# Laying the normalised activations out anew in place, by cycles of chunk copies, instead of building them three times

## The chip, the cores and the metric

The kernel runs on one core of one Trainium2 chip. The metric is the device time of one execution in microseconds, the median over several executions.

## The reference, cut to what matters

One layer takes 2048 prompt tokens and 64 decode tokens (8 sequences of 8). The activations are normalised and multiplied by one wide matrix; of the product, twelve heads of q, k and v go to attention. The heads are in three groups of four, with dilations 1, 4 and 16: a query sees its own token and 128 earlier ones, each `dil` apart. The three groups are merged by the softmax of their log-sums. A gated linear recurrence runs beside it, and both branches are gated, projected and added to the input.

```
u = rms_norm(x, g_norm);  z = u @ w_in            # xa, ga, q, k, v, gb, gm
for g, dil in enumerate((1, 4, 16)):              # per class t % dil, blocks of 128 tokens
    s = q_blk @ [k_prev, k_blk].T * scale + bias[dist]     # band of 129
    o[g], lse[g] = softmax(s) @ [v_prev, v_blk], logsumexp
ob = sum_g softmax_g(lse)[g] * o[g];  yb = (ob * silu(gb)) @ w_attn_proj
h = scan(a * h + b);                  ya = (h * silu(ga)) @ w_lru_proj
y = x + (sig(gm1) * ya + sig(gm2) * yb) @ w_out
```

## The kernel before, in words

All matmuls are in float32r with operands split into a high and a low part. The normalised activations stand transposed in SBUF as `RH` and `RL` (high and low part): 128 partitions, 8 slices of the model dimension, 2112 token columns. They are 16 blocks of 128 prompt tokens and one of 64 decode tokens.

**Order of work.** The program is written out by hand in the order in which each engine is to run it. The attention loop (L536) goes over 204 units: twelve heads, groups 2, 1, 0 (dilations 16, 4, 1), and per head 16 prompt blocks and one decode block. Below, *head n* is the n-th in this order (heads 0 to 3 have dilation 16, 4 to 7 dilation 4, 8 to 11 dilation 1), and `ph` is the unit's place in its head. A unit runs through stages spread over four iterations: projection `z` of the block (`stage_a`, 24 matmuls in three parts), then norms (`stage_b1` to `b3`; the scale `rs` comes from two small POOL operations, L347 and L348), transposes of k and q (`stage_c`), scores and softmax (`stage_d`), transposes of the probabilities (`stage_e`), their product with v (`stage_f`), and the sum into tile `o` (`stage_g`, DVE), which SP writes to the DRAM buffer `Osc` (L435). After a head's last block, SP gathers the softmax statistics from `Osc` into `STt` (L437).

**Layout.** A block must be 128 tokens of one class modulo `dil`, in order. So before groups 1 and 0 the whole array is made anew during the last head of the group before (heads 3 and 7): per unit one block of x is loaded (L225), multiplied by scale and weight (`x_mul`, L241, two DVE operations), transposed on PE (`x_tr`, L248, eight 128x128 transposes) and split into `RH` and `RL` (L94 on ACT, L95 on DVE, two of each).

**Beside it.** The decode path's scores against the K cache (`kgo`: two DVE reductions L179 per step, 128 steps for a group) run inside the loop: group 2's in heads 4 to 6, group 1's in heads 8 to 11. The K tiles come over SP's queue. Weights are loaded a head ahead in four `wraw` buffers (L305) and split (L312 to L324); the bias band `T3` is read from DRAM (L298, L299).

After the loop come the attention gates (L534), the recurrence (L763 with L864 and L926; eight blocks), gate matmuls, and the output projections (L1425, L1481, L1513).

Of the kernel before, what the change touches and what calls it, by code (L numbers as in the profile page):

```python
# [42 lines left out]
def program(tc, I, O, C, upto=99, debug=False):  # L43
# [21 lines left out]
    RS = sd("RS", [SEQ])  # L65
# [18 lines left out]
    RH = rp.tile([128, 8, NT], F32R, name="RH")  # L84
    RL = rp.tile([128, 8, NT], F32R, name="RL")
# [117 lines left out]
    xrs = ap_.tile([128, 2, 17], F32, name="xrs")  # L203
    xt = {}

    def x_open():
# [3 lines left out]
        if G.again:  # L210
            x_load(1)
# [3 lines left out]
    def xv(j):  # L215
        if j == 16:
            return I["x_sample"].rearrange("b t d -> (b t) d")
        d = DIL[G.xg]
        r, n = divmod(j, 16 // d)
        return I["x_prompt"][0, n * 128 * d + r:min(n * 128 * d + r + 128 * d, SEQ):d, :]  # L220

    def x_load(j):
        if j < (17 if G.xg == 2 and not G.again else 16):
# [3 lines left out]
    def x_norm(j):  # L227
# [4 lines left out]
        POOL.tensor_tensor(xrs[0:p, 0, j:j + 1], ss[0:p, 1:2], neghalf[0:p, 0:1], ALU.pow)  # L232

    def x_scales():
        dma(raw(RS, 0, [[16, 128], [1, 16]]), xrs[:, 0, 0:16])
        dma(xrs[:, 1, 0:16], raw(RS, 0, [[4, 128], [1, 4], [512, 4]]))
        dma(xrs[:, 0, 0:16], raw(RS, 0, [[1, 128], [128, 16]]))

    def x_mul(j, a=0, b=D):
        p = 128 if j < 16 else NS  # L240
        DVE.scalar_tensor_tensor(xt[j][0:p, a:b], xt[j][0:p, a:b], xrs[0:p, G.xg % 2, j:j + 1], G.gn[0:p, a:b], ALU.mult, ALU.mult)  # L241

    def x_tr(j, i):
# [115 lines left out]
    def stage_b3(u):  # L359
# [7 lines left out]
        if u.smp:  # L367
            dma(SK[u.g, :, :, u.h, :], u.kvo[0:m])
            dma(QS[u.g, :, u.h * HD:(u.h + 1) * HD], u.qn[0:m, :])
        elif u.out is not None:  # L370
            dma(u.out, u.kvo)
# [12 lines left out]
    def stage_d(u):  # L384
# [11 lines left out]
        u.o = ap_.tile([128, 130], F32, name="o", tag="o", bufs=3)  # L396
# [1206 lines left out]
```

## Time and profile before

| | us |
|---|---|
| median of 3 runs | 2517.61 (2517.22 to 2520.73) |
| the profiled execution | 2513.91 |
| its span, first to last instruction | 2512.1 |
| PE busy | 2477.1 (99%) |
| DVE busy | 1544.1 (61%) |
| ACT busy | 1083.5 (43%) |
| POOL busy | 565.1 (22%) |

Busy shares are taken over the span. Matmuls are pipelined, so that several are in flight at once and the durations of single ones add up to more than PE's time. DMA-issuing instructions of SP are not counted as busy.

### The profile page before, as it was taken

Reading aid. Unit: us, or ns where it says so; the run is one execution under the profiler, and the core shown is the slowest. Engines: PE = TensorE matmul, PEld = TensorE weight load, DVE = VectorE, ACT = ScalarE, POOL = GpSimd, SP = SyncE. Lnnn points to the kernel's source line nnn. Section 1 sums busy time; section 2 is a strip of 40 time slices with the busy share of each in tenths; the row PEclk is TensorE's granted clock in tenths of the full one; section 3 lists DMA queues with packets and bytes.
Section 4 is the critical chain, followed back from the end, with each engine's and each line's share of the span. In section 5 each row is a group of like instructions: output and inputs, shape, how many; then the busy total and the mean of one; then the engine's idle time right before and its main releaser. Section 6 shows DMA issues by size and latency. Waiting matters only on the chain.

```text
span 2512.1 us, 44593 instructions
## 1 busy us (share of the span) xinstructions
PE 2477.1 (99%) x15178; PEld 2333.8 (93%) x15178; DVE 1544.1 (61%) x4805; ACT 1083.5 (43%) x3318; POOL 565.1 (22%) x901
## 2 busy tenths in 40 slices
PE   8999999999999999999999999999999999999999
PEld 7999999999999999999998989998998899989988
DVE  6744687777786777746567767766776633423323
ACT  5634454443444434444355566546566511211110
POOL 3423322222212212223324334340000112200000
PEclk9999999999999999999999999999999999999999
DMA  5453565555553443426644433445654489533332
GB/s 146 119 131 106 148 186 148 167 172 144 163 171 112 132 122 99 124 81 203 202 155 139 147 103 120 143 126 187 201 195 154 151 262 328 169 118 122 110 120 67
DMA packets 310824, 376.30 MB, mean 150 GB/s; under 512 B 55360, under 2 KB 254943, under 8 KB 307756
## 3 DMA queue, kind: packets, MB, share of 16 engines
q1 hardware_dynamic: 283604, 336.12, 44.2%
q0 software_dynamic: 15472, 20.02, 3.0%
q10 hardware_dynamic: 11520, 17.31, 1.9%
q8 instruction: 120, 1.97, 0.3%
q14 instruction: 108, 0.88, 0.1%
HBM read 295.45 MB, written 168.33 MB: 185 GB/s over the span
## 4 chain that ended last, share of the span: by engine, by line
PE 87%; DMA 4%; DVE 3%; ACT 2%; issue 2%; POOL 1%; SPq 0%; ACTq 0%; POOLq 0%; DVEq 0%
PE z L336 28%; PE zt L763 28%; PE zt L1481 8%; PE zt L1513 7%; PE zt L1425 3%; PE zt L534 3%; PE zga L891 2%; PE trx L248 1%; PE op L428 1%; PE S L406 1%; PE tre L416 1%; PE trc L376 1%; DMA wr<-in_w_in 1%; DMA xt<-in_x_prompt 1%; PE trc L377 1%
## 5 line engine op out<-in xcount | busy, mean ns | idle before, releaser
L336 PE MATMUL z<-w,RH 128*128 128x384 f32 (+1 forms) x3088 | 888.9, 349 | 4.9 <-POOL w L317 1.8
L763 PE MATMUL zt<-RH,wz 128*128 128x384 f32 (+2 forms) x2560 | 695.5, 354 | 0.0
L336 PEld LDWEIGHTS z<-w,RH 128*128 128x128 f32 (+1 forms) x3088 | 553.1, 188 | 14.8 <-POOL w L317 5.9
L336 PE MATMUL z<-w,RL 128*128 128x384 f32 x1544 | 520.3, 337 | 0.1
L763 PEld LDWEIGHTS zt<-RH,wz 128*128 128x128 f32 x2560 | 463.3, 189 | 43.1 <-issue 1.0
L763 PE MATMUL zt<-RL,wz 128*128 128x384 f32 (+2 forms) x1280 | 452.5, 353 | 0.0
L336 PEld LDWEIGHTS z<-w,RL 128*128 128x128 f32 x1544 | 291.3, 189 | 0.8 <-DVE RL L95 0.5
L763 PEld LDWEIGHTS zt<-RL,wz 128*128 128x128 f32 x1280 | 241.3, 189 | 22.2
L179 DVE CUSTOM_DVE_ANT_0 kjk<-kt,qs 128x128 bf16<-128x128 f32 x768 | 227.5, 296 | 37.0 <-DMA kt<-in_cache_kv_w 13.8
L408 ACT ACTIVATE P<-P,o 128x128 f32<-128x128 f32 (+1 forms) x192 | 88.9, 463 | 312.8 <-DVE o L407 312.8
L345 ACT ACTIVATE jk<-z 128x128 bf16<-128x128 f32 (+1 forms) x408 | 113.0, 277 | 249.9 <-PE trc L376 185.0
L347 POOL TENSOR_SCALAR ss<-ss 128x2 f32<-128x2 f32 (+1 forms) x204 | 45.1, 221 | 705.2 <-ACT jk L345 666.7
L95 DVE TENSOR_TENSOR KQ<-trc,KQ 128x256 fp32r<-128x256 f32 x192 | 81.4, 424 | 198.2 <-ACT KQ L94 198.2
L1481 PEld LDWEIGHTS zt<-y1t,w_wlo 128*128 128x128 f32 x1536 | 190.3, 191 | 0.6
L1481 PE MATMUL zt<-y1t,w_wlo 128*128 128x256 f32 (+1 forms) x1536 | 190.6, 286 | 0.0
L1513 PE MATMUL zt<-w_wo,mt 128*128 128x512 f32 x672 | 162.0, 395 | 0.0
L1513 PEld LDWEIGHTS zt<-w_wo,mt 128*128 128x128 f32 x672 | 126.0, 188 | 30.7
L348 POOL TENSOR_TENSOR rs<-ss,neghalf 128x2 f32<-128x2 f32 (+1 forms) x204 | 142.8, 700 | 17.0
L94 ACT CAST mt<-g 128x256 fp32r<-128x256 f32 x72 | 27.2, 388 | 191.2 <-DVE g L1484 176.0
L434 DVE TENSOR_REDUCE o<-op 128x128 f32<-128x256 f32 x192 | 80.5, 419 | 44.8 <-PE op L429 44.7
L1515 DVE TENSOR_TENSOR xr<-zt,xr 128x512 f32<-128x512 f32 (+1 forms) x34 | 23.5, 692 | 137.2 <-PE zt L1513 132.5
L1150 ACT ACTIVATE v<-v,P 128x128 f32<-128x128 f32 x256 | 80.1, 390 | 47.1 <-DVE SCk L179 23.2
(291 smaller groups left out, 4247.1 us busy)
## 6 DMA issues: line engine op xcount, KB each, us to landing
out_kv_s<-in_cache_kv_w SPq DMA_DIRECT2D x176, 480.0 KB
xt<-in_x_prompt SPq DMA_DIRECT2D x48, 512.0 KB
wr<-in_w_in SPq DMA_DIRECT2D x96, 192.0 KB
kt<-in_cache_kv_w SPq DMA_DIRECT2D x128, 128.0 KB
wzr<-in_w_in SPq DMA_DIRECT2D x32, 512.0 KB
v<-in_cache_kv_w SPq DMA_DIRECT2D x128, 128.0 KB
Osc<-o SPq DMA_DIRECT2D x192, 65.0 KB
ot<-Osc SPq DMA_DIRECT2D x32, 390.0 KB
```

The costliest lines, as they stand in the source:

```text
L95: eng.tensor_sub(l, src, h.bitcast(F32))
L179: DVE.tensor_tensor_reduce(jk, kts[q.tile][:, c], qts[t][:, c], 1.0, 0.0, ALU.mult, ALU.add, q.SC[:, o:o + 1])
L336: PE.matmul(u.z[0:m, :], (RH, RL, RH)[p][:, k, u.cols], Wt[(u.g, u.h), k][:, (0, 0, 1)[p], :], start=(i == 0), stop=(i == 23))
L345: ACT.activation(jk[0:m, :], z[0:m, i * 128:(i + 1) * 128], AF.Square, accum_out=u.ss[0:m, i:i + 1])
L348: POOL.tensor_tensor(u.rs[0:m, :], u.ss[0:m, :], neghalf[0:m, :], ALU.pow)
L408: ACT.activation(u.P[:, 0:n], u.P[:, 0:n], AF.Exp, bias=u.o[:, 128:129], scale=-1.0, accum_out=u.o[:, 129:130])
L434: DVE.tensor_reduce(u.o[:, 0:128], u.op.rearrange("p a b -> p b a"), AX.X, ALU.add)
L534: PE.matmul(z[0:m, 0:256], (RH, RH, RL)[p][:, k, j * 128:j * 128 + m], wb[c * 8 + k][:, (0, 1, 0)[p], :], start=(i == 0), stop=(i == 23))
L763: PE.matmul(z[:, 0:n], w[:, (0, 1, 0)[p], k, :], (RH, RH, RL)[p][:, k, c0:c0 + n], start=(i == 0), stop=(i == 23))
L1150: ACT.activation(v2s[n][:, h], v2s[n][:, h], AF.Copy, scale=P2[:, h, n:n + 1])
L1481: PE.matmul(z[:, 0:n], wl[k][:, (0, 1, 0)[p], f, :], y1s[c * 8 + k][:, (0, 0, 1)[p], 0:n], start=(i == 0), stop=(i == 23))
L1513: PE.matmul(z[0:m, :], ms_[k][:, (0, 0, 384)[p] + o:(0, 0, 384)[p] + o + m], wo[k][:, (0, 1, 0)[p], e * 4:(e + 1) * 4, :].rearrange("p k c ...
```

## The change

The array is loaded, scaled and transposed once. `RH` and `RL` become two views of one tile `RX`. Blocks start in the order of dilation 16 with classes 0, 4, 8, 12, 1, 5, ... For dilation 4, and later for dilation 1, chunks of 32 columns (of all 16 slices of high and low part: 512 elements in each partition) are moved in place: 24 exchanges of two chunks (three copies each, 72) in head 3, and 20 cycles of three chunks (four copies each, 80) in head 7 and the first units of head 8. Each cycle starts with a POOL copy into one of four spare tiles; in exchanges DVE makes the other two copies, in cycles of three ACT, DVE and ACT make the other three. Up to five copies are issued in a unit (two, two, one).

The tokens of a block stay permuted within it. The bias band is therefore read with permuted rows and its columns are permuted by a POOL copy (`bias_p`), two units after the read and some units earlier than before; k and v outputs go out in parts; `Osc` holds rows in the permuted order of dilation 1; the recurrence un-permutes on ACT's way into `xpad` and permutes on POOL's product L926; x and y are read and written with permuted rows. The `o` tiles of dilation 4 are written by four POOL DMAs (32 rows each), issued one unit later, or at once after a head's last block. The K-cache steps begin at iterations 73 and 149 instead of 71 and 139, and the second lot runs two per place throughout.

```diff
-    RH = rp.tile([128, 8, NT], F32R, name="RH")
-    RL = rp.tile([128, 8, NT], F32R, name="RL")
+    RX = rp.tile([128, 2, 8, NT], F32R, name="RX")
+    RH, RL = RX[:, 0], RX[:, 1]
...
-        return I["x_prompt"][0, n * 128 * d + r:min(n * 128 * d + r + 128 * d, SEQ):d, :]
+        return I["x_prompt"][0, j // 4 + 4 * (j % 4):SEQ:16, :]
...
+    def chunk(g, blk, n):
+        v = RX.rearrange("p s k t -> p (s k) t")[:, :, blk * 128:blk * 128 + 128]
+        if g == 1:
+            return v[:, :, n * 32:n * 32 + 32]
+        return v.rearrange("p k (c n i) -> p k c n i", c=4, n=4)[:, :, :, n]
...
+    def queue(g, blk):
+        for c in cycles(g, blk):
...
+            def first(c=c, t=t):
+                v = G.xp.tile([128, 16, 32], F32R, name="mv", tag="mv", bufs=4)
+                t.append(v if g == 1 else v.rearrange("p k (c i) -> p k c i", c=4))
+                cp(POOL, t[0], chunk(g, *c[-1]))
+            fs = [first]
+            for n in range(len(c) - 1, 0, -1):
+                fs.append(lambda n=n, c=c: cp((ACT, DVE)[n % 2], chunk(g, *c[n]), chunk(g, *c[n - 1])))
+            fs.append(lambda c=c, t=t: cp((DVE, ACT)[len(c) % 2], chunk(g, *c[0]), t[0]))
+            moves.extend((min(b for b, n in c), f) for f in fs)
+        moves.sort(key=lambda m: m[0])
...
+    def bias_p(g, h):
+        if g != 2:
+            A = PA[g]
+            t = ap_.tile([128, 384], F32, name="T3", tag="T3", bufs=2)
+            POOL.tensor_copy(t.rearrange("p (n a b) -> p n a b", a=A, b=128 // A), Tt[g, h].rearrange("p (n b a) -> p n a b", a=A, b=128 // A))
...
-        u.o = ap_.tile([128, 130], F32, name="o", tag="o", bufs=3)
+        u.o = ap_.tile([128, 130], F32, name="o", tag="o", bufs=4)
...
+    def flush_o():
+        if G.late:
+            G.late()
+            G.late = None
     def stage_g(u):
...
+        flush_o()
         DVE.tensor_reduce(u.o[:, 0:128], u.op.rearrange("p a b -> p b a"), AX.X, ALU.add)
-        dma(Osc[u.g, u.tok, u.h, :], u.o)
...
+            G.late = lambda: [POOL.dma_start(raw(Osc, b + (u.blk % 4 * 512 + (4 * a + u.r) * 8) * st, [[128 * st, 4], [st, 8], [1, 130]]), u.o[a * 32:a * 32 + 32]) for a in range(4)]
         if u.last:
+            flush_o()
...
-            kgo(2 if i < 136 else 1 + (i % 2 == 0))
+            kgo(2)
...
-            if i > 50 and i // 17 in (3, 7) and ph:
-                x_mul(ph - 1, D // 2, D)
-                x_tr(ph - 1, 0)
+            move(2)
             stage_a(u, 1)
...
-                x_tr(ph - 1, 1)
-                x_load(ph + 1)
+            move(2)
             stage_a(u, 2)
+            if i // 17 in (3, 7) and ph < 16:
+                queue(1 if i < 68 else 0, ph)
...
-                x_mul(ph, 0, D // 2)
+            move(1)
...
-        ACT.copy(xpad[:, 3 + c0:3 + c0 + npr], z[:, 0:npr])
+        ACT.copy(xpad[:, 3 + c0:3 + c0 + npr].rearrange("p (n k x) -> p n x k", k=8, x=16), z[:, 0:npr].rearrange("p (n x k) -> p n x k", k=8, x=16))
```

## Rows read from the trace of the kernel before

**Rows 1.** The page, section 1: busy us, share of the span, instructions.
```profile
PE 2477.1 (99%) x15178; PEld 2333.8 (93%) x15178; DVE 1544.1 (61%) x4805; ACT 1083.5 (43%) x3318; POOL 565.1 (22%) x901
```
**Rows 2.** The page, section 4: the chain that ended last, shares by line.
```profile
PE z L336 28%; PE zt L763 28%; PE zt L1481 8%; PE zt L1513 7%; PE zt L1425 3%; PE zt L534 3%; PE zga L891 2%; PE trx L248 1%; PE op L428 1%; PE S L406 1%; PE tre L416 1%; PE trc L376 1%; DMA wr<-in_w_in 1%; DMA xt<-in_x_prompt 1%; PE trc L377 1%
```
**Rows 3.** Windows, line 376 alone (one per unit): stretch, length, PE busy (count).
```profile
213.25:298.49 85.24, 4.61 (x17) 2.35 (x17) 1.00 0.44 121
```
**Rows 4.** Windows, heads 2 to 7: PE, PEld, DVE, ACT, POOL busy, clock, DMA.
```profile
213.25:298.49 85.24, 84.94 (x525) 82.63 (x524) 43.98 (x157) 35.51 (x162) 25.88 (x54) 1.00 0.44 121
298.49:399.07 100.58, 98.17 (x639) 94.31 (x638) 81.34 (x214) 50.50 (x191) 25.93 (x53) 1.00 0.61 175
399.07:488.30 89.23, 89.10 (x565) 87.52 (x564) 65.48 (x317) 36.97 (x160) 21.08 (x42) 1.00 0.57 168
488.30:579.47 91.17, 89.66 (x566) 87.55 (x565) 69.09 (x333) 37.07 (x160) 20.95 (x42) 1.00 0.53 158
579.47:672.31 92.84, 90.21 (x573) 88.36 (x572) 63.88 (x289) 38.36 (x162) 21.43 (x42) 1.00 0.54 162
672.31:776.84 104.53, 103.32 (x687) 100.40 (x686) 81.96 (x202) 53.14 (x191) 21.78 (x42) 1.00 0.53 152
```
**Rows 5.** Windows, tile trx alone (the x transposes), heads 3 and 7.
```profile
298.49:399.07 100.58, 18.59 (x120) 12.59 (x120) 21.20 (x31) 17.30 (x30) 1.00 0.61 175
...
672.31:776.84 104.53, 18.32 (x120) 13.06 (x120) 21.19 (x31) 17.30 (x30) 1.00 0.53 152
```
**Rows 6.** Timeline into iteration 116: start, us, engine, line, operation, [idle before, releaser].
```profile
644.72 1.01 DVE L95 TENSOR_TENSOR w<-wr,w 128x384 fp32r<-128x384 f32 x1
...
646.41 0.19 POOL L347 TENSOR_SCALAR ss<-ss 128x2 f32<-128x2 f32 x1 [1.10 <-ACT jk L345]
...
646.62 0.42 DVE L95 TENSOR_TENSOR KQ<-trc,KQ 128x256 fp32r<-128x256 f32 x1 [0.89 <-ACT KQ L94]
646.69 0.69 POOL L348 TENSOR_TENSOR rs<-ss,neghalf 128x2 f32<-128x2 f32 x1
...
647.60 0.34 DVE L363 SCALAR_TENSOR_TENSOR kvo<-z,rs,gk 128x128 f32<-128x128 f32 x1
647.63 0.28 PE L399 MATMUL S<-KQ 128*128 128x256 f32 x1
...
650.59 0.27 PE L376 MATMUL trc<-ident,kvo 128*128 128x128 f32 x1
```
**Rows 7.** Groups by line and form: count | busy us, mean ns | idle before.
```profile
L179 DVE CUSTOM_DVE_ANT_0 kjk<-kt,qs 128x128 bf16<-128x128 f32 x768 | 227.5, 296 | 37.0 <-DMA kt<-in_cache_kv_w 13.8 <-DMA qs<-QS 1.2 <-DMA out_h_s<-hs 0.2
L95 DVE TENSOR_TENSOR RL<-trx,RH 128x512 fp32r<-128x512 f32 x96 | 66.4, 691 | 39.4 <-ACT RH L94 39.0
L1154 DVE COPY V<-v 128x512 f32<-128x512 f32 x1 | 0.4, 408 | 0.0
L882 ACT CAST xh<-xc 128x512 fp32r<-128x512 f32 x16 | 10.0, 625 | 33.2 <-DVE xc L873 33.2
L907 POOL TENSOR_TENSOR a<-rr 128x512 f32<-128x512 f32 x16 | 16.3, 1042 | 56.3 <-ACT rr L905 48.9 <-issue 7.4
L926 POOL TENSOR_TENSOR sgl<-sgl,tt 128x512 f32<-128x512 f32 x16 | 24.5, 1533 | 32.4 <-DVE tt L925 32.4
L1135 POOL DMA_DIRECT2D PSC<-pp x8 | 4.4, 572 | 53.7 <-DVE pp L1132 53.7
L758 POOL DMA_DIRECT2D Y<-yt x16 | 12.1, 756 | 10.0 <-ACT yt L94 6.1 <-ACT ob L739 3.0 <-ACT sg L712 0.8
```
**Rows 8.** DMA issues: operation, count, KB each, median us to landing.
```profile
PSC<-pp POOLq DMA_DIRECT2D x8, 16.0 KB, 3.9
```
**Rows 9.** The chain in order of time, end of head 4: start, us, what.
```profile
489.90 4.80 DMA Osc<-o
```
**Rows 10.** Windows, one block of the recurrence: same columns as rows 4.
```profile
1291.67:1343.24 51.57, 51.57 (x272) 46.97 (x271) 36.63 (x50) 30.93 (x54) 20.15 (x20) 1.00 0.43 140
```
**Rows 11.** Source view of line 144: durations ns min/median/max, first and last start.
```profile
L144 SPq DMA_DIRECT2D qs<-QS x16: 605/606/662, 775.3 to 786.2; - x16
```

More of the change, by code (lines that the diff above doesn't have):

```diff
@@ L217, in xv @@
             return I["x_sample"].rearrange("b t d -> (b t) d")
[L218 to L220 removed]
+        return I["x_prompt"][0, j // 4 + 4 * (j % 4):SEQ:16, :]
     def x_load(j):
[L223 removed]
+        if j < 17:
             xt[j] = G.xp.tile([128, D], F32, name="xt", tag="xt", bufs=2)
@@ L253, in x_tr, with cycles, move, cp @@
             POOL.tensor_copy(XS[:, i * 4:i * 4 + 4, 1], RL[s].bitcast(F32))
+    PA = (16, 4)
+    moves = []
+    def chunk(g, blk, n):
[3 more added lines that the diff above has]
+        return v.rearrange("p k (c n i) -> p k c n i", c=4, n=4)[:, :, :, n]
+    def cycles(g, blk):
+        out = []
+        for x in range(4):
+            for y in range(4):
+                for z in range(4):
+                    if g == 1:
+                        c = [(4 * x + y, z), (4 * x + z, y)]
+                        ok = y > z
+                    else:
+                        c = [(4 * x + y, z), (4 * y + z, x), (4 * z + x, y)]
+                        ok = (x, y, z) == max((x, y, z), (y, z, x), (z, x, y)) and not x == y == z
+                    if ok and max(b for b, n in c) == blk:
+                        out.append(c)
+        return out
+    def move(n):
+        for _ in range(n):
+            if moves:
+                moves.pop(0)[1]()
+    def queue(g, blk):
+        for c in cycles(g, blk):
+            t = []
+            engs = (ACT, DVE, POOL)
+            def cp(e, o, i):
+                (ACT.copy if e is ACT else e.tensor_copy)(o, i.bitcast(F32))
+            def first(c=c, t=t):
[8 more added lines that the diff above has]
+        moves.sort(key=lambda m: m[0])
     gws = ExitStack()
@@ L369, in stage_b3 @@
             dma(QS[u.g, :, u.h * HD:(u.h + 1) * HD], u.qn[0:m, :])
+        elif u.out is not None and u.g == 2:
+            dma(u.out, u.kvo)
         elif u.out is not None:
-            dma(u.out, u.kvo)
+            A = PA[u.g]
+            if u.g == 1:
+                for a in range(4):
+                    dma(u.out[a::4], u.kvo[a * 32:a * 32 + 32])
+            else:
+                for b in range(8):
+                    (dma if b % 2 else POOL.dma_start)(u.out[b * 16:b * 16 + 16], u.kvo[b::8])
     def stage_c(u):
@@ L628, in program @@
         if nh:
-            if ph == 7 and nh[1] == 0:
+            if ph == 4 and nh[1] == 0:
                 bias_0(nh[0])
-            if ph == 9 and nh[1] == 0:
+            if ph == 6 and nh[1] == 0:
                 bias_a(nh[0])
-            if ph == 10:
+            if ph == 7:
                 bias_c(*nh)
-            if ph == 12:
+            if ph == 9:
                 bias_b(*nh)
+            if ph == 11:
+                bias_p(*nh)
             if ph == 11:
```

68 lines of the change are left out of this document (37 added, 31 removed).

## The prediction

> **What bounds the kernel now.** I read the page's busy shares first [rows 1]: PE 99%, the next engine, DVE, 61%. The chain of waits [rows 2] says the same from the other side: nearly all its links are PE matmuls, and the x transposes (trx, L248) are one of them with 1%. A share over 2512 us doesn't tell what a stage would give, so I cut the attention loop by heads. Line 376 runs once per unit; a window from its first start in one head to its first in the next holds 17 of them [rows 3], so such a window is one head's worth of units. Head 2 and head 3 do the same attention work, and head 3 builds a new layout: 85.24 against 100.58 us [rows 4]. In both PE is busy nearly throughout (84.94 and 98.17) at a clock of 1.00. Head 7, the other one with a layout, takes 104.53 against 89.23, 91.17 and 92.84 in heads 4 to 6, which have the same attention work and carry K-cache steps instead. So a head goes at PE's pace, and work taken off PE shortens it, unless another engine then comes last. The other engines, by the same rows: without a layout DVE has 43.98 of 85.24 us (head 2), with one 81.34 of 100.58 (head 3). The second number is near enough to the span that DVE has to be watched.
>
> **What is removed.** Two times 16 blocks of eight transposes. The view of their tile shows about 120 of them in each of the windows [rows 5] (the window's edges and missing records account for the rest), with 21.2 us of DVE and 17.3 us of ACT for the splits, and beside them two x multiplications per block on DVE. What they cost PE I take from the windows and not from the matmuls' own durations, which overlap: head 3 should go at head 2's time, 100.58 - 85.24 = 15.3 us less. For head 7 the measure is heads 4 and 5, mean (89.23 + 91.17) / 2 = 90.2, so 14.3 us less. Head 6 I leave out of the mean because it holds the longest DMA-bound stretch of the three (its PE is busy 90.21 of 92.84). Sum removed: 29.6 us. This is the whole expected gain; everything below asks what of it is lost.
>
> **The moves in head 3.** 72 copies: 24 on POOL, 48 on DVE, about five per unit from place 1 on. No row has a copy of this shape into float32r. The nearest for DVE is a plain copy of 128x512 at 0.408 us, the upper bound a two-input operation of that size at 0.691 [rows 7]. I take 0.41: the copy has one input, as the row has. DVE in head 3 is then head 2's 43.98 + 48 x 0.41 = 63.7 us of 85.24; by the bound 77.1. Both fit. POOL: 24 copies by 1.04 us (its two-input operation of 128x512, bounds 0.4, as DVE's copy, and 1.53 [rows 7]) on top of 25.88: 51 of 85.24, at most 62.6. The copies run for blocks whose columns PE is done with, and a block is needed again only a head later: by the order in which the moves are sorted, the last of them are issued at iteration 68, where block 0 is read, and belong to blocks 13 to 15. PE waits for none of them if each engine keeps within its unit. Cost taken: 0, bounds 0 and, if DVE were the bound at 0.691 with a third of its time lost in waiting for POOL, 77.1 x 4/3 - 85.2 = 17.6.
>
> **The moves in heads 7 and 8.** 80 copies, spread over iterations 123 to 142: 20 POOL, 40 ACT, 20 DVE. ACT by 0.625 each [rows 7]: 25 us over 20 units, 1.25 per unit, where heads 4 to 6 leave ACT at 37 of 89 us [rows 4]. DVE has no K-cache steps here. Cost taken: 0; what could go wrong is the first rival.
>
> **The results of dilation 4.** SP loses 64 writes, POOL gains 256. The nearest row is eight POOL writes of 32 runs of 512 bytes at 0.572 us each; larger ones stand at 0.756 [rows 7]. Four times 0.572 is 2.3 us per unit, and POOL's own two small operations are 0.19 and 0.69 [rows 6]: 3.2 us of a unit of 5.25 (89.23 / 17 [rows 4]). What is queued behind these writes on POOL is the next unit's norm, and DVE's kvo (L363) waits for it. Slack there: kvo and the like operation after it end by 647.60 + 2 x 0.34 = 648.3, PE wants them at 650.59 [rows 6], 2.3 us later. Inside a head the writes wait for nothing, because their tile was summed a unit earlier; they end well before the next norm. At a head's end eight come together, the last four only after the sum, and the norm behind them slips by up to 2.3 us: just the slack. Also SP's gather into `STt` waits until these have landed. Before, that wait was 4.80 us from SP's late issue [rows 9]; POOL's landing row is 3.9 us [rows 8] after up to 2.3 us of issuing, so the gather goes about 1.4 us later, and K tiles queue behind it on SP. I take 0.3 us for each of the four head ends, 1.2 in all. Bounds: a gain of 5.6 us, if SP without its `Osc` writes brings the K tiles in time and heads 5 and 6 come down to head 4's 89.23 (1.9 + 3.6); a loss of 1.9 for each, what head 5 lost to such a place.
>
> **The K-cache steps.** Group 2's start two iterations later but must still end at iteration 115. Per head there are 48 calls (four steps at places 1 and 2, three at 3 to 15, one at 0). Iterations 73 to 115 hold 33 + 48 + 42 = 123 of 128, so five are flushed at the end of 115: ten DVE reductions at 0.296 [rows 7], 3.0 us. There DVE ends a weight split at 645.73 and starts KQ at 646.62, which PE needs at 647.63 [rows 6]. With the flush KQ starts near 648.7, 2.1 late; it had 647.63 - 647.04 = 0.6 to spare. PE loses 1.5 us, and it can't be won back. Group 1's steps go from 2.5 to three per unit; heads 4 to 6 already carry three, with DVE at 65.48 of 89.23, so 0. At iteration 146 sixteen query loads of 0.606 us [rows 11] go into SP's queue just ahead of the next head's weight loads: 9.7 us later, against a use three units (16 us) on. 0, bounds 0 and 3.
>
> **The rest.** The recurrence: a block is 51.57 us with PE busy for all of it, ACT 30.93, POOL 20.15 [rows 10]. The permuted product L926 (1.53 us) and the permuted copy into `xpad` have no row. Even at twice the time, 5 x 1.53 = 7.7 us more for POOL, it has 27.8 of 51.57 and nothing that PE reads in the same block waits for L926. 0, bounds 0 and 8 (a microsecond per block). `bias_p` is one POOL copy per head in eight heads, two units after its data were asked for: 0. Outputs of k and v in parts and permuted rows of x and y move the same bytes: 0, bounds 0 and 3, and SP sheds 32 loads of x.
>
> **The sum.** -29.6 + 1.2 + 1.5 = -26.9 us: the profiled execution of 2513.91 us (span 2512.1 and 1.8 around it) becomes 2487.0. The median of the runs, 2517.61, is 3.7 higher than that execution; on its scale the time is 2490.7.
>
> **A rule that speaks against it.** POOL's rows are 0.572 us per small write, eight in a row [rows 7]. The Trainium skill, "SBUF — State Buffer", section "SBUF: two separate sides", says that a DVE copy of 32-bit data within SBUF shuts POOL out of a port the two share, so that a DMA issued from POOL can't write its descriptors until the copy is over. No run here shows the two together. By that rule the writes of heads 4 to 6 stay as they are, since DVE copies nothing there; in heads 7 and 8 the 20 DVE copies could each hold POOL up for 0.41 us, 8 us spread over 20 units, and the sum stays. It is a reason to give the second rival more than I would otherwise.
>
> **The rivals.**
> *The cycles hold each other up in heads 7 and 8.* The copies of a cycle run one after the other on POOL, ACT, DVE, ACT; a POOL copy behind four writes ends 2.3 + 1.04 = 3.3 us after the norm, 1.0 later than the slack of 2.3 that I read, and the copies behind it stand in ACT's and DVE's queues ahead of the next unit's work. For it: POOL has the least room just there. Against: its place is after the norm, and a unit has 5.25 us. At 1.0 us in each of the 20 units the gain shrinks by 20 to 2510.7; in half of them 2500.7. Chance 0.15.
> *POOL becomes the bound in dilation 4.* If one write costs more than (5.25 - 0.88) / 4 = 1.1 us, each of the 68 units of heads 4 to 7 goes at POOL's pace. The gain is used up at 26.9 / 68 = 0.40 us per unit, that is at 1.2 us per write; at 1.5 a unit is 6.9, 110 us more, and the time 2602. For it: 256 such writes, one after the other, are more than any row shows, and the rule above. Against: eight in a row at 0.572. Chance 0.07, slower.
> *The transposes were free.* If PE's time in heads 3 and 7 was set by DVE (81.34 and 81.96 busy) and the moves put DVE back there, the change does not do what it says, and the time stays within 5 us of 2517.6. Against: PE is busy 98.17 of 100.58. Chance 0.04.
> *The K tiles come in time.* The gain of 5.6 us above, and the 1.2 not lost: 2483.9. For it: SP has 64 writes fewer to wait for. Chance 0.09.
>
> **How the numbers follow.** The forecast has the remaining 0.65, with an own range of 2486 to 2497 (the bounds of 3 us each, one of them met). I take 2490.7 as the time. The range of 2483 to 2504 takes in the last rival and the lighter half of the first. What this kernel's measurement can tell from no change is about 0.2%, 5 us: faster has 0.65 + 0.09 + 0.14, same 0.01 + 0.04, slower 0.07.
>
> **What would show it.** Right: no trx rows after the first head, windows of head 3 near 85 and of head 7 near 90; POOL's writes of o near 0.57 us each; PE idle between units as now; heads 5 and 6 as before within 2 us; a step of 1.5 us after iteration 115. Wrong: windows of heads 4 to 6 above 93 with kvo waiting for POOL's norm (second rival); PE or ACT waiting for tile RX or mv in heads 7 and 8 (first); head 3 near 100 with DVE busy throughout (third).

## The result and the profile after

The changed kernel takes 2530.49 us (median of 4 runs, 2527.47 to 2536.57) against 2517.41 for the kernel before in the same series: ratio 1.0055, interval 1.0037 to 1.0073. It is slower, where 2490.7 was forecast: 39.8 us off and outside the range. A second series of five runs gave 2536.56 (2531.84 to 2539.22), ratio 1.0085 (1.0071 to 1.0099). The kernel before kept to 2516.0 to 2517.4 in all series, the changed one did not; its level is known to some 6 us. The profiled execution is one of 2536.57, 22.7 above the one profiled before.

Section 1 of the page answers to [rows 1]:
```profile
PE 2471.1 (97%) x14922; PEld 2319.4 (92%) x14922; DVE 1500.3 (59%) x4745; ACT 1082.2 (43%) x3294; POOL 770.8 (30%) x1233
```
PE is busy 6.0 us less, with 256 fewer instructions, and the span is 22.6 us longer: PE's idle time has grown by 28.6 us, from 35.0 to 63.6. The windows, cut at the line that stood in [rows 3] (now line 443), for heads 2 to 9 show where (columns as in [rows 4]):
```profile
214.27:298.68 84.41, 84.13 (x517) 81.85 (x516) 41.75 (x153) 34.31 (x160) 26.43 (x55) 1.00 0.45 120
298.68:385.58 86.90, 85.28 (x519) 81.90 (x518) 61.88 (x201) 34.68 (x161) 41.28 (x77) 1.00 0.44 119
385.58:476.36 90.78, 89.67 (x565) 87.76 (x564) 63.31 (x286) 37.13 (x160) 57.47 (x103) 1.00 0.55 156
476.36:569.37 93.01, 90.41 (x565) 87.75 (x564) 70.11 (x333) 37.05 (x160) 60.00 (x108) 1.00 0.55 157
569.37:668.24 98.87, 93.81 (x565) 90.59 (x564) 67.66 (x316) 36.95 (x160) 60.32 (x109) 0.97 0.50 143
668.24:769.37 101.13, 94.09 (x567) 89.11 (x566) 48.48 (x155) 52.23 (x189) 68.74 (x121) 0.98 0.30 82
769.37:869.94 100.57, 94.97 (x577) 92.22 (x576) 52.63 (x200) 44.21 (x172) 28.19 (x55) 0.97 0.35 102
869.94:963.18 93.24, 91.11 (x577) 89.21 (x576) 69.29 (x330) 37.80 (x160) 22.28 (x44) 1.00 0.41 118
```
Head 3 went from 100.58 to 86.90, as forecast. Head 7 fell only from 104.53 to 101.13, and every other head from 4 to 10 grew in this execution; head 8, 90.91 before, has 100.57. In head 7 PE is idle for 7.0 of 101.13 us, and no engine is near its limit (the next, POOL, has 68.74). So these are stalls, not a new bound. PE's waits from head 3 to the end of the loop (what waited, for what: us in total, times, longest):
```profile
PE S L466 <- DVE KQ L94: 7.8, 4, 2.9
PE z L395 <- ACT w L371: 7.7, 8, 1.8
PE S L473 <- ACT KQ L93: 5.0, 4, 2.3
PE z L395 <- POOL w L376: 1.6, 5, 0.4
PE trc L443 <- DVE kvo L422: 1.5, 2, 0.8
PE S L454 <- ACT kqs L447: 1.5, 1, 1.5
PE tre L483 <- ACT P L475: 1.5, 2, 0.7
```
The same view of before holds 8.9 us in all. Here it is 26.6. Tile `w`, the split weights, has 9.3 of it in place of 2.2. At the end of several of these stalls, or just behind them, PE ran at the lower of its two clock levels. A window just after the stall at 757.21 us shows it (granted clock 0.51, next to the last three figures):
```profile
757.40:760.70 3.30, 3.30 (x12) 3.11 (x12) 2.20 (x7) 1.73 (x8) 1.33 (x3) 0.51 0.21 68
```
The clock records hold nine such stretches between 600 and 2210 us, eight of 3.4 us and one of 6.8; before, there is one, of 6.8. That is 27 us more at half speed, some 13.6 us of work. They are inside the windows above. What one costs can be read off head 6, which has the same four waits in three executions of this loop: 95.78 us without such a stretch (the second series), 97.15 with one (the run with the plain recurrence, below), 98.87 with two (above). So a stretch costs some 1.5 us, and a stall of 2.5 us can cost a head 4:
```profile
570.21:665.99 95.78, 90.68 (x565) 87.70 (x564) 67.64 (x316) 37.06 (x160) 60.00 (x108) 1.00 0.52 148
570.15:667.30 97.15, 92.16 (x565) 89.18 (x564) 67.52 (x316) 36.91 (x160) 59.88 (x108) 0.98 0.50 146
```

After the loop (1142.9 us; before 1135.4) 15 us more are lost. The blocks of the recurrence have 52.16 us in place of 51.57 [rows 10]:
```profile
1328.42:1380.58 52.16, 51.84 (x272) 46.92 (x271) 37.48 (x50) 32.50 (x53) 21.31 (x22) 1.00 0.42 138
```
and a stage of the last projection (L1563) waits once for `y1t`, 2.9 us, with a half-clock stretch behind it.

### The profile page after: what moved, and what is told of

The parts are those of the page before. It is cut to its first block, busy times and chain, and to the rows that moved or that the text cites. A ratio compares the mean times of both kernels' runs of the same rounds, so it can differ in the third digit from the quotient of the medians.

```text
span 2534.7 us, 44453 instructions
## 1 busy us (share of the span) xinstructions
PE 2471.1 (97%) x14922; PEld 2319.4 (92%) x14922; DVE 1500.3 (59%) x4745; ACT 1082.2 (43%) x3294; POOL 770.8 (30%) x1233
## 5 line engine op out<-in xcount | busy, mean ns | idle before, releaser
L395 PE MATMUL z<-w,RX 128*128 128x384 f32 x4632 | 947.6, 347 | 11.9 <-ACT w L371 8.0
L395 PEld LDWEIGHTS z<-w,RX 128*128 128x128 f32 x4632 | 788.4, 190 | 23.4 <-ACT w L371 9.5
L841 PE MATMUL zt<-RX,wz 128*128 128x384 f32 (+2 forms) x3840 | 746.6, 354 | 0.0
L841 PEld LDWEIGHTS zt<-RX,wz 128*128 128x128 f32 x3840 | 670.5, 189 | 65.4 <-issue 1.0
L1563 PEld LDWEIGHTS zt<-y1t,w_wlo 128*128 128x128 f32 x1536 | 191.9, 193 | 4.3 <-ACT y1t L93 3.1
L1563 PE MATMUL zt<-y1t,w_wlo 128*128 128x256 f32 (+1 forms) x1536 | 192.6, 288 | 3.2 <-ACT y1t L93 2.9
L516 POOL DMA_DIRECT2D Osc<-o x256 | 153.8, 606 | 8.7 <-DVE o L509 4.2
L94 POOL TENSOR_TENSOR y1t<-yr,y1t 128x256 fp32r<-128x256 f32 (+1 forms) x32 | 25.2, 787 | 289.3 <-ACT y1t L93 289.3
L614 PE MATMUL zt<-wb,RX 128*128 128x256 f32 (+1 forms) x816 | 103.2, 284 | 0.0
L614 PEld LDWEIGHTS zt<-wb,RX 128*128 128x128 f32 (+1 forms) x816 | 98.0, 187 | 0.1
## 6 DMA issues: line engine op xcount, KB each, us to landing
wr<-in_w_in SPq DMA_DIRECT2D x96, 192.0 KB
```

The source lines that it names most:

```text
L94: eng.tensor_sub(l, src, h.bitcast(F32))
L395: PE.matmul(u.z[0:m, :], (RH, RL, RH)[p][:, k, u.cols], Wt[(u.g, u.h), k][:, (0, 0, 1)[p], :], start=(i == 0), stop=(i == 23))
L516: G.late = lambda: [POOL.dma_start(raw(Osc, b + (u.blk % 4 * 512 + (4 * a + u.r) * 8) * st, [[128 * st, 4], [st, 8], [1, 130]]), u.o[a * 3 ...
L614: PE.matmul(z[0:m, 0:256], (RH, RH, RL)[p][:, k, j * 128:j * 128 + m], wb[c * 8 + k][:, (0, 1, 0)[p], :], start=(i == 0), stop=(i == 23))
L841: PE.matmul(z[:, 0:n], w[:, (0, 1, 0)[p], k, :], (RH, RH, RL)[p][:, k, c0:c0 + n], start=(i == 0), stop=(i == 23))
L1563: PE.matmul(z[:, 0:n], wl[k][:, (0, 1, 0)[p], f, :], y1s[c * 8 + k][:, (0, 0, 1)[p], 0:n], start=(i == 0), stop=(i == 23))
```

## The experiments

Theory A: the stalls are separate, each with a cause of its own in the change, and the clock adds to each. Theory B: one cause, POOL's 256 result writes, and a repair only moves the wait. Each run's windows are in the table behind the last experiment. The first four runs are of one series, which did not hold the changed kernel itself; their totals are set against its 2530.49, and as its level is known to some 6 us only, so is what they gained.

**The K steps opened at iteration 68**, not 70, so that nothing is flushed at 115.
```diff
-        if i in (70, 146) and upto > 1:
+        if i in (68, 146) and upto > 1:
```


> The changed kernel, with the K-cache steps of dilation 16 opened at iteration 68 instead of 70, so that none is left to flush at the end of iteration 115. Theory A (PE stands still at several separate places, each with a cause of its own, and the clock drops after each): the 2.48 us wait of PE for KQ in iteration 116 and the 3.4 us at half clock behind it go, so head 6 goes from 98.9 to about 94.8 us and the whole is 4 us faster, about 2526. Theory B (one cause, POOL's 256 writes, holds up everything in heads 4 to 8): the wait in iteration 116 stays, since POOL's queue is what is late, and the time stays at 2530.

2530.63 us, ratio 1.0064 (1.005 to 1.0078). The wait at iteration 116 is gone and head 6 has 93.36, in place of 98.87 and 95.78 in the two profiles of the changed kernel. So the local effect is theory A's. Its total, 2526, is a miss: against 2530.49 nothing was gained. The profiled execution doesn't say why, since it is the slowest of the six (2541.32; its heads 8 to 10 hold 27.3 us of half-clock stretches, the changed kernel's 10.2).

**The parts of the k and v outputs behind the weight loads of a head's end**, on the same engines.
```diff
-                for a in range(4):
-                    dma(u.out[a::4], u.kvo[a * 32:a * 32 + 32])
...
+            def parts():
+                if u.g == 1:
+                    for a in range(4):
+                        dma(u.out[a::4], u.kvo[a * 32:a * 32 + 32])
...
+            G.parts = parts
...
                 w_load(nh, k + 4)
+        if G.parts:
+            G.parts()
```


> The changed kernel, with the k and v outputs that go out in four or eight parts issued later in the iteration, behind the next head's last two weight loads. Theory A: PE's waits for ACT w L371 at the ends of heads 4, 5, 6, 8, 9 and 10 (0.94, 0.71, 0.96, 1.52, 1.80, 1.45 us, 7.4 in all) go, with two drops of the clock behind them (3.4 us at half speed each, 1.7 us lost): about 10 us faster, 2520. Theory B: those waits are the weight loads' own time behind POOL, and the time stays within 3 us of 2530.

2521.08 us, ratio 1.0020 (1.0011 to 1.0029). The waits for `w` are down to 0.4 us in all, and heads 9 and 10 have 90.84 each, below the 91.18 and more of before. As theory A has it. SP's queue at the end of head 4 in the changed kernel (start, us taken, line, operation):
```profile
463.37 1.76 SPq L435 DMA_DIRECT2D out_kv_p<-kvo  x4
465.23 0.96 SPq L366 DMA_DIRECT2D wr<-in_w_in  x2
```
and at the same place in the kernel before:
```profile
476.68 0.40 SPq L371 DMA_DIRECT2D out_kv_p<-kvo  x1
477.20 0.97 SPq L307 DMA_DIRECT2D wr<-in_w_in  x2
```
Four parts take SP 1.76 us where one write took 0.40, and the last two weight loads of the next head start behind them.

**First copy of each cycle of three on DVE** in place of POOL, where it stood behind the result writes.
```diff
-                cp(POOL, t[0], chunk(g, *c[-1]))
+                cp(POOL if g == 1 else DVE, t[0], chunk(g, *c[-1]))
```


> The changed kernel, with the first copy of each cycle of three chunks on DVE instead of POOL (the cycle is then DVE, ACT, DVE, ACT). Theory A: a cycle no longer stands in ACT's queue waiting for a POOL copy behind four writes; PE's waits for KQ in heads 7 and 8 (1.6, 1.1, 2.3, 1.5 and 2.9 us, with two clock drops) mostly go: heads 7 and 8 from 101.1 and 100.6 to about 92 to 95 each, the whole 12 us faster, 2518. Theory B: POOL's writes themselves delay the norms there, and heads 7 and 8 gain at most 4 us.

2528.63 us, ratio 1.0047 (1.0034 to 1.006). Heads 7 and 8 went from 201.7 to 193.5 together, twice what theory B allows, but 2.3 us of the wait at iteration 136 stayed, so POOL's queue is not all of it. The total misses theory A's 2518; in the profiled execution heads 9 and 10 hold 13.7 us of half-clock stretches, the changed kernel's 3.4.

**The recurrence without its two permutations** (it then runs over tokens in permuted order).
```diff
-        ACT.copy(xpad[:, 3 + c0:3 + c0 + npr].rearrange("p (n k x) -> p n x k", k=8, x=16), z[:, 0:npr].rearrange("p (n x k) -> p n x k", k=8, x=16))
+        ACT.copy(xpad[:, 3 + c0:3 + c0 + npr], z[:, 0:npr])
...
-            POOL.tensor_mul(sv, sv, tt[:, c0:c0 + npr].rearrange("p (n k x) -> p n x k", k=8, x=16))
+            POOL.tensor_mul(sgl[:, c0:c0 + npr], sgl[:, c0:c0 + npr], tt[:, c0:c0 + npr])
```


> The changed kernel, with the recurrence's copy into xpad and its product with the gate in plain order, that is without undoing and redoing the permutation of the tokens; the recurrence is left to run over permuted tokens. Theory A: the copy (1043 ns against 579) and the product (1792 against 1533) go back, PE's seven waits of 0.36 us for xh go, and a block takes 51.57 us again instead of 52.18: 4 to 5 us faster, 2526. Theory C (what was lost behind the attention loop is chance of the profiled execution): no change, 2530.

2529.55 us, ratio 1.005 (1.0038 to 1.0062). Seven waits of about 0.35 us for tile `xh` are gone and blocks are back at 51.57. By the total it is inconclusive.

**The first three repairs together.**

> The three repairs at once: K steps of dilation 16 opened at iteration 68, the parts of the k and v outputs issued behind the last weight loads of a head's end, first copy of each cycle of three on DVE. Theory A (each stall has a cause of its own, and part of what one repair wins locally went into stretches at half clock behind the stalls that were left): the windows show all three at once, head 6 from 98.9 to 92-93, heads 7 and 8 together from 201.7 to 190-194, ends of heads 9 and 10 as with the parts moved alone (90.8). If the single runs' totals simply add (0, -9.4, -2 against the changed kernel's 2530.5) the time is 2519; if the local gains of 5.5 and 8.2 come out once few stalls are left, it is 2507. Theory B (POOL's 256 result writes hold everything up, and a repair only moves the wait): above 2519, with new waits on POOL in the same heads.

2510.0 us, ratio 0.9974 (0.9966 to 0.9983): faster than before. The windows show all three local gains at once: head 6 has 92.9, heads 7 and 8 together 192.0, heads 9 and 10 each 90.9. One half-clock stretch is left between head 3 and the end of the loop, where the changed kernel has six. Whether the repairs are worth more together than singly isn't shown: against 2530.5 they were worth 0, 9.4 and 2 singly and 20.5 together, but against the 2536.6 of this run's own series it would be 5.9, 15.5, 7.9 and 26.6. Theory B as the one cause is out by this run: POOL's writes were all there. What part they have in heads 7 and 8 is seen two runs below.

**The copies left out.**
```diff
-                moves.pop(0)[1]()
+                moves.pop(0)
```


> The copies that build the layouts are left out altogether (so heads of dilation 4 and 1 compute on tokens in the wrong order; all else is done as in the changed kernel). This prices them. Theory A: head 3 from 86.9 to 84.5-86, head 7 from 101.1 to about 93, head 8 from 100.6 to about 93 (heads 9 and 10, with the same K steps and the same parts of k and v, have 93.2 and 94.6); time 2530.5 - 16 = 2514. Rival C (heads 7 and 8 are long because the K steps of group 1 now run there at three per unit and sixteen query loads go into SP's queue, not because of the copies): head 8 stays above 98, time above 2524.

2519.51 us, ratio 1.0016 (1.0004 to 1.0028).
```profile
300.17:385.48 85.31, 85.02 (x519) 81.88 (x518) 41.75 (x153) 34.76 (x161) 26.21 (x54) 1.00 0.44 121
...
666.69:759.15 92.46, 90.81 (x568) 87.78 (x567) 42.28 (x141) 37.63 (x161) 59.63 (x108) 1.00 0.33 90
759.15:855.63 96.48, 93.41 (x577) 90.70 (x576) 50.33 (x194) 37.90 (x160) 24.68 (x49) 0.98 0.37 106
```
These are heads 3, 7 and 8. The copies cost 86.90 - 85.31 = 1.6 us in head 3 and (101.13 + 100.57) - (92.46 + 96.48) = 12.8 in heads 7 and 8. Against the changed kernel in the same series the time is 17.0 lower, where theory A said 16. Head 8 is below rival C's 98 but above theory A's 93; what it has over head 9 (93.0, with the same wait for `w`) is a wait for KQ of 0.8 us at iteration 150, one iteration after the second lot of K steps begins, and a half-clock stretch. So rival C is out for the larger part; that the K steps make the 0.8 us isn't shown.

**The four result writes by SP**, on top of the parts behind the weight loads.
```diff
-            G.late = lambda: [POOL.dma_start(raw(Osc, b + (u.blk % 4 * 512 + (4 * a + u.r) * 8) * st, [[128 * st, 4], [st, 8], [1, 130]]), u.o[a * 32:a * 32 + 32]) for a in range(4)]
+            G.late = lambda: [dma(raw(Osc, b + (u.blk % 4 * 512 + (4 * a + u.r) * 8) * st, [[128 * st, 4], [st, 8], [1, 130]]), u.o[a * 32:a * 32 + 32]) for a in range(4)]
```


> As the run with the k and v parts behind the weight loads (2521.1), and the four result writes per unit of dilation 4 issued by SP in place of POOL, one unit later as before. Theory A (POOL's eight writes at a head's end delay the norm, about 1.5 us of PE waits in heads 5 and 6 each, and POOL's writes ahead of the first copy of a cycle are part of heads 7's and 8's stalls): those waits go, heads 5 and 6 shorter by 1 to 2 each, head 7 by 1 to 3; 2516 to 2518. Theory B (the 256 POOL writes are the cause of most of it): 2510 or less. Rival D (SP's queue is the tighter one: four writes of about 0.45 us per unit stand ahead of weight loads and K tiles): heads 4 to 6 longer by 2 or more each, 2525 or more.

2545.57 us, ratio 1.0118 (1.01 to 1.0135), rival D: heads 4 to 6 have 98.44, 105.40 and 110.35. DVE's waits there:
```profile
DVE kjk L178 <- DMA kt<-in_cache_kv_w: 39.9, 13, 8.3
```
In the changed kernel the same waits are 2.3 us. SP has no room for these writes beside the K tiles; of the two engines POOL was the right one. In heads 7 and 8, which have no K tiles before iteration 149, the same run shows what the writes do on POOL: 95.63 and 92.07 us, where the parts alone moved gave 101.4 and 97.1, so 10.8 less. PE's waits in these two heads are 3.5 us in place of 10.6, and the 2.3 at iteration 136 is the bulk of what is left. POOL's writes are thus most of the stalls of heads 7 and 8, though not of the others.

**The changed kernel again.**

> The changed kernel as it is, in the same series as the three above, to have its time and its windows a second time. Theory A: 2530.5 within 2; the same waits at the same places (heads 4 to 10, iteration 116, heads 7 and 8), and the stretches at half clock behind some of them, not all at the same places. If the waits stand at other places, the windows of one profile can't be used to say what a part costs.

2536.56 us, the result of the second series; theory A's 2530.5 within 2 was missed by 6. The waits stand at the same places (iterations 85, 105, 116, 119, 130 to 138, 150 to 187), save those of head 5, which are missing; heads agree within 0.5 us except 4 to 6, by up to 3.1. So one profile's windows can be read, those three with that margin. Half-clock stretches behind the same waits are partly at other places.

**The permuted rows alone, in the kernel before.**
```diff
-    xsrc = lambda t0: I["x_sample"].rearrange("b t d -> (b t) d") if t0 >= SEQ else I["x_prompt"][0, t0:t0 + 128, :]
+    xsrc = lambda t0: I["x_sample"].rearrange("b t d -> (b t) d") if t0 >= SEQ else I["x_prompt"][0, t0:t0 + 128, :].rearrange("(k x) d -> x k d", k=8)
```
(and the same for `ydst`)

> One part of the change alone, put into the kernel before: x is read for the residual sum and y is written in the permuted row order (the sum then pairs the wrong tokens; nothing else is changed). Theory A, one more term that the prediction set to 0: SP's loads and writes of these rows take 0.55 to 0.61 us in place of 0.35 to 0.38, the write lands about a microsecond later, and the loads of y1 behind it on SP come late once: a PE wait for y1t of 1 to 3 us near 2165, with a stretch at half clock behind it, and 0.8 at the very end: 2516.3 + 3 to 5 = 2519 to 2521. Rival: the wait for y1t comes from the recurrence or from chance: no wait, 2516 to 2517. The wait of OT for Z (0.6 to 2.7 us in every trace with the change, none before) should not appear here if the change makes it; if it appears, it is chance.

2521.77 us against 2516.68, ratio 1.0019 (1.001 to 1.0028): +5.1, at the upper edge of what theory A gave. SP's queue before the wait:
```profile
2172.89 0.62 SPq L1524 DMA_DIRECT2D out_yp<-xr  x1
2177.48 0.55 SPq L1468 DMA_DIRECT2D xr<-in_x_prompt  x1
2178.12 7.29 SPq L1391 DMA_DIRECT2D yr<-Y  x4
```
and what PE waited for in that stretch:
```profile
PE zt L1481 <- ACT y1t L94: 2.7, 1, 2.7
```
The kernel before, at the same place:
```profile
2171.34 0.38 SPq L1524 DMA_DIRECT2D out_yp<-xr  x1
2174.21 0.33 SPq L1468 DMA_DIRECT2D xr<-in_x_prompt  x1
2174.64 5.67 SPq L1391 DMA_DIRECT2D yr<-Y  x4
```
The load of `xr` takes the buffer that the write leaves; with permuted rows it can start 4.59 us after the write was issued instead of 2.87, and the loads of `yr` queue behind it. Behind the wait PE ran 6.8 us at half clock. The wait of `OT` for `Z` (2.2 us here; 0.9 to 2.7 in the traces with the change, none in the one of before) appears in this kernel and in the next, whose edits have nothing in common, so I count it to no part. The one trace of before is of 2513.91, below its median, and its other executions may well have the wait too; that isn't shown, and if they don't, each of the two totals holds some 2 us of it.

**The k and v parts alone, in the kernel before.**
```diff
-            dma(u.out, u.kvo)
+            if u.g == 2:
+                dma(u.out, u.kvo)
+            elif u.g == 1:
+                for a in range(4):
+                    dma(u.out[a * 32:a * 32 + 32], u.kvo[a * 32:a * 32 + 32])
+            else:
+                for b in range(8):
+                    (dma if b % 2 else POOL.dma_start)(u.out[b * 16:b * 16 + 16], u.kvo[b * 16:b * 16 + 16])
```


> Another part alone in the kernel before: the k and v outputs of dilation 4 and 1 written in four and eight parts by the same engines as in the changed kernel, same content and places, nothing else changed. Theory A: at the ends of heads 4 to 6 and 8 to 10 the last two weight loads stand behind the parts on SP, PE waits 0.7 to 1.8 us for tile w at each, half-clock stretches behind some of them: six ends by 1.5 to 2.2, 2516.3 + 9 to 13 = 2525 to 2529. Rival: the parts alone do no harm (SP has time here, since the change's other work isn't there): below 2519, no waits for w.

2526.97 us, ratio 1.0043 (1.003 to 1.0056): +10.3, with the waits that theory A named:
```profile
PE z L336 <- ACT w L312: 6.6, 7, 1.7
PE z L336 <- POOL w L317: 2.6, 7, 0.5
```

**Six repairs.** Beside the three: the last writes of a head go out a unit later like the others, the copy into `xpad` runs in the order of its output, and `xr` is loaded behind the y1 loads of both row blocks.
```diff
-        ACT.copy(xpad[:, 3 + c0:3 + c0 + npr].rearrange("p (n k x) -> p n x k", k=8, x=16), z[:, 0:npr].rearrange("p (n x k) -> p n x k", k=8, x=16))
+        ACT.copy(xpad[:, 3 + c0:3 + c0 + npr].rearrange("p (n k x) -> p n k x", k=8, x=16), z[:, 0:npr].rearrange("p (n x k) -> p n k x", k=8, x=16))
...
-            xr_load(xseq.index(t0 // 128) + 2)
+            nx.append(xseq.index(t0 // 128) + 2)
+            if c == 7 or o == 128:
+                for j in nx:
+                    xr_load(j)
```


> The three repairs that gave 2510.0 and three more: at the end of a dilation 4 head the last four result writes go out a unit later like the others (the gather into STt with them); the copy into xpad runs over its output in natural order and reads PSUM with a stride, in place of the other way round; the loads of x for the next rows go onto SP behind the y1 loads of both row blocks. Theory A: waits for kvo and P at iterations 88 and 105 (1.5 us each) go, the wait for y1t (2.1 us) goes, recurrence blocks 52.18 go back to 51.57 if the strided write was what made the copy 1.04 us (7 x 0.6 = 4.3): 2510.0 - 3 - 2 to 4 - 4 = 2499 to 2501. Rival 1: a strided read of PSUM is as slow as a strided write, then 2503 to 2505. Rival 2: gains are lost to new waits or to the clock, 2508 or more.

2496.46 us, ratio 0.9929 (0.9917 to 0.9942), somewhat better than theory A's 2499. The waits for `kvo`, `P` and `y1t` are gone; heads 4 to 6 have 89.4 to 89.5. The copy into `xpad` in the changed kernel, by the view of its tile (duration ns min/median/max):
```profile
L942 ACT COPY xpad<-zt x40: 585/842/1075, 1262.6 to 1639.7; 128x512 f32<-128x512 f32 x16, 128x384 f32<-128x384 f32 x16, 128x256 f32<-128x256 f32 x8
```
and in this one:
```profile
L955 ACT COPY xpad<-zt x40: 349/481/610, 1232.6 to 1607.1; 128x512 f32<-128x512 f32 x16, 128x384 f32<-128x384 f32 x16, 128x256 f32<-128x256 f32 x8
```
The same elements, written with a stride of 16, take 842 ns; read with a stride of 8 and written in order, 481, as a plain copy did before (481). The block is at 51.81, so 0.24 us of the 0.61 is left; PE no longer waits for `xh`, and what holds it isn't known (the permuted product on POOL is still there).

**Cycles interleaved**, on top of the six: an entry of `moves` is now a whole cycle, and two cycles are worked off in turn.
```diff
-                moves.pop(0)[1]()
+                m = moves[G.tog % min(2, len(moves))]
+                G.tog += 1
+                m[1].pop(0)()
+                if not m[1]:
+                    moves.remove(m)
```


> As the six repairs, and the copies of two cycles taken in turn, so that a copy and the one that reads what it wrote no longer follow each other on the queues. Theory A (what is left in heads 7 and 8 is the chain inside a cycle across engines, each in-order queue holding the next unit's KQ behind a copy that waits): waits of PE for KQ at iterations 131 to 139 and 150 (5.2 us, and a half-clock stretch) shrink to under 2, heads 7 and 8 some 3 to 5 shorter than in the run before: 2495 to 2498. Rival (it is the sheer number of copies on ACT and DVE, or the weight splits at iteration 136, not the chain): heads 7 and 8 within 1 of it, the same time.

2489.54 us (2486.94 to 2492.59), ratio 0.9896 (0.9882 to 0.9909): 27.1 below the kernel before, and below theory A's 2495 to 2498. PE's waits in heads 7 and 8, with the six repairs:
```profile
PE S L474 <- ACT KQ L93: 3.4, 3, 2.2
PE S L467 <- DVE KQ L94: 0.8, 1, 0.8
PE S L455 <- ACT kqs L448: 0.5, 1, 0.5
```
and with this one:
```profile
PE S L478 <- ACT KQ L93: 1.0, 2, 0.5
```
Heads 7 and 8 have 91.90 and 92.00 with as many copies as before: what cost the time was the order, not the number.

Lengths of heads 3 to 10 by the windows (one profiled execution each, us), and the median:

| kernel | 3 | 4 | 5 | 6 | 7 | 8 | 9 | 10 | median |
|---|---|---|---|---|---|---|---|---|---|
| before | 100.6 | 89.2 | 91.2 | 92.8 | 104.5 | 90.9 | 91.5 | 91.2 | 2516 to 2517 |
| after | 86.9 | 90.8 | 93.0 | 98.9 | 101.1 | 100.6 | 93.2 | 94.6 | 2530.5 |
| after again | 86.9 | 92.2 | 91.2 | 95.8 | 101.5 | 101.0 | 93.4 | 94.6 | 2536.6 |
| no flush | 86.9 | 90.7 | 92.8 | 93.4 | 102.2 | 104.1 | 95.7 | 95.6 | 2530.6 |
| parts behind weights | 86.9 | 89.4 | 91.8 | 95.8 | 101.4 | 97.1 | 90.8 | 90.8 | 2521.1 |
| first copy on DVE | 86.9 | 93.2 | 91.3 | 95.7 | 97.6 | 95.9 | 96.4 | 95.7 | 2528.6 |
| recurrence plain | 86.9 | 91.1 | 92.9 | 97.2 | 101.3 | 100.9 | 95.2 | 93.0 | 2529.6 |
| three together | 86.9 | 89.4 | 91.8 | 92.9 | 97.7 | 94.3 | 90.9 | 90.9 | 2510.0 |
| no copies | 85.3 | 90.8 | 92.9 | 97.5 | 92.5 | 96.5 | 93.0 | 94.5 | 2519.5 |
| writes by SP | 86.9 | 98.4 | 105.4 | 110.4 | 95.6 | 92.1 | 90.9 | 90.9 | 2545.6 |
| rows alone, in before | 101.1 | 89.5 | 90.3 | 91.9 | 104.5 | 90.9 | 92.0 | 90.7 | 2521.8 |
| parts alone, in before | 101.0 | 91.1 | 91.1 | 93.4 | 105.2 | 92.7 | 94.3 | 92.8 | 2527.0 |
| six repairs | 86.9 | 89.4 | 89.5 | 89.4 | 97.2 | 92.8 | 90.9 | 90.8 | 2496.5 |
| interleaved | 86.9 | 89.4 | 89.5 | 89.4 | 91.9 | 92.0 | 90.9 | 90.8 | 2489.5 |

## Why the prediction was wrong

The gain was judged rightly, and most of what eats it was set to nothing without looking at the queue that it stands in.

| term | forecast | measured | by |
|---|---|---|---|
| head 3, copies included | -15.3 | -13.7 | windows |
| heads 0 to 2 | 0 | +0.3 | windows (+1.9 in head 0) |
| head 7, copies left out | -14.3 | -12.1 | windows |
| copies in heads 7 and 8 | 0 | +12.8 | copies left out |
| k and v outputs in parts | 0 (0 to 3) | +10.3 | that part alone |
| permuted rows of x and y | in the same bounds | +5.1 | that part alone |
| flush at iteration 115 | +1.5 | +2.4 to +5.5 | head 6 with K steps opened at 68, against the two profiles |
| recurrence | 0 (0 to 8) | +4.3 | 7 blocks by 0.61 |
| result writes at head ends, K tiles | +1.2 | +0.7 | heads 5 and 6 with three repairs, to before |

The misses add up to 37 to 40 us. The medians miss the forecast by 39.8, and the profiled execution, from which most windows come, misses its own (2487.0) by 49.6. So the account holds the bulk, but that it closes on the median is in part luck: the terms come from different kernels and executions, overlap a little (head 7's windows hold waits for `w`), and each carries the clock's part with it. Step by step:

*What is removed* held: no `trx` rows after head 0, head 3 near 85. Without copies head 7 has 92.46 where 90.2 was forecast.

*The moves in head 3: 0* was near: they cost 1.6. "PE waits for none of them" failed in one place, iteration 67, where four DVE copies stand ahead of KQ and PE waits 1.32 us for it, in every version that has the copies.

*"Outputs of k and v in parts and permuted rows of x and y move the same bytes: 0"* is the step that failed worst, by 15.4 us, over half of what the change was to bring. Bytes were the wrong measure. What counts is how long SP is taken up by issuing, and what stands behind: at a head's end the last two weight loads, on which PE waits; at the last projection the loads of y1. The prediction reads no row of SP's queue at either place ([rows 6] hold PE, DVE and POOL only); what a step is put ahead of was asked of the `Osc` writes, the gather and the query loads, not of these.

*The moves in heads 7 and 8: 0* failed, and the first rival (0.15) names the mechanism: a cycle's copies wait for each other across queues, and the next unit's KQ stands behind one that waits. Its price of 10 to 20 us holds the 12.8. Its start, POOL copies behind the result writes, is the larger part (8.2 us less with the first copy on DVE, 10.8 with the writes on SP); the chain of copies across the in-order queues is the rest, and interleaving removes both. ACT's queue into iteration 136 of the changed kernel shows it (start, us, [idle before, releaser]); S waits for this KQ until 757.21:
```profile
753.31 0.62 ACT L286 CAST RX<-RX 128x512 fp32r<-128x512 f32 x1 [1.08 <-POOL mv L286]
753.84 0.51 ACT L93 CAST w<-wr 128x384 fp32r<-128x384 f32 x1
755.64 0.62 ACT L286 CAST RX<-mv 128x512 fp32r<-128x512 f32 x1 [1.29 <-DVE RX L286]
756.28 0.48 ACT L624 COPY zl<-z 64x384 f32<-64x384 f32 x1
756.78 0.37 ACT L93 CAST KQ<-trc 128x256 fp32r<-128x256 f32 x1
```
ACT stood idle for 1.08 and 1.29 us ahead of two copies with KQ queued behind them. The durations were cheaper than assumed (a POOL copy has a median of 617 ns, not 1.04 us; DVE's 428). Busy time on the engine could not show this; the order in its queue did.

*The flush* was found, with 3.0 us on DVE. PE's wait came out at 2.48 against 1.5, and half-clock stretches weren't in the sum: head 6 lost 2.4 us in the execution without one and 5.5 in the one with two, the second of them behind a wait for `w`.

*The results of dilation 4.* A write takes 606 ns on the mean over 256, against 0.572 assumed; the second rival (a bound above 1.1) is out.
```profile
L516 POOL DMA_DIRECT2D Osc<-o x256 | 153.8, 606 | 8.7 <-DVE o L509 4.2 <-issue 3.7
```
Two errors cancelled: eight writes at a head's end cost heads 5 and 6 waits for `kvo` and `P` of 1.5 us each, five times the 0.3 taken; and the fourth rival's gain was there, as those heads fall to 89.54 and 89.36 with the six repairs, the 89.23 that it named. (That SP's shorter queue is its cause, and not the later gather or the K steps opened earlier, isn't shown.) The port shared by DVE and POOL shows in the trace, and costs next to nothing. Ten of the 256 writes overlap a DVE copy of the moves. Seven last 589 to 600 ns, like the others. Three, with a copy that begins 0.16 to 0.21 us into the write, last 760, 689 and 722 ns, and each ends 117 to 119 ns behind the copy. A write of either kind, each with the DVE copy that it overlaps:
```profile
715.35 0.60 POOL L516 DMA_DIRECT2D Osc<-o  x1
715.40 0.42 DVE L286 CAST RX<-RX 128x512 fp32r<-128x512 f32 x1
729.37 0.76 POOL L516 DMA_DIRECT2D Osc<-o  x1
729.58 0.43 DVE L286 CAST RX<-RX 128x512 fp32r<-128x512 f32 x1
```
In the interleaved kernel eight writes end so, 117 to 126 ns behind a copy. The Trainium skill's "SBUF — State Buffer", section "SBUF: two separate sides", has a POOL write held until the copy is over; the trace agrees for these, and the three together lost some 0.4 us, well inside the 8 us that the prediction set for it.

*The recurrence* lies inside its bounds. Of 0.61 us per block, 0.37 go with ACT's strided write; the rest is open.

*The clock* is in no term, though the trace of before has a half-clock stretch of 6.8 us at the end of its longest wait (4.3 us, near 1929). What a stall costs beyond its own length was never asked.

What stays open: why the changed kernel's median differs by 6 us between two series while that of before doesn't. The granted clocks of the runs go with it (0.993 to 0.996 in the first series, 0.993 to 0.994 in the second), and by their means the clock would make some 3 of the 6 us, an estimate; why it fell more often isn't shown. The later series ran on another chip than the single repairs, and the chip of the first is not on record, so a difference between chips is not excluded; the kernel before agrees between them within 1.4 us. Open too are 7.6 us behind the loop that the interleaved version still has over the kernel before (1384.4 against 1376.8 from the loop's end). The recurrence explains some 1.7 and the permuted last write 0.8; waits of PE that are longer or new there (`OT` for `Z` 2.2 with a half-clock stretch, `OT` for `vt` 5.6 against 4.3, `try` for `ob` 2.3 against 1.0) make up the rest, and their causes were not looked for.

## What to carry to other kernels

A DMA that is cut into parts moves the same bytes but holds the queue that issues it for longer (here 1.76 us against 0.40): ask what is queued behind it at that place, above all the loads that the next stage starts with. Chains of dependent copies across in-order engines are best interleaved, so that no queue holds urgent work behind a copy that waits. Where PE is the bound, a short stall is priced with the half-clock stretch that can follow it, and single repairs are judged by their windows, with the changed kernel itself measured in the same series if their totals are to count.

## What the runs showed of the hardware

On ACT, from PSUM into SBUF, a stride on the writing side took 842 ns against 481 with the stride on the reading side. POOL's product of 128x512 with permuted operands took 1792 ns in place of 1533 [rows 7]. Stalls of PE of 0.9 to 2.9 us were often, not always, followed by 3.4 us at half clock, which cost some 1.5 us each. A POOL write into which a DVE copy of 128x512 within SBUF fell ended 117 to 119 ns behind that copy, up to 165 ns later than the median write of 595 ns.
